# Differential attention: two 64-row score products on the halves of the array in place of one product with a block-diagonal key

## The chip, the core and the metric

The program runs on one core of a Trainium2 chip, as one launch. Its engines are TensorE (PE; PEld is its weight load), VectorE (DVE), ScalarE (ACT), GpSimd (POOL), and SyncE (SP), which here only starts DMAs. Each engine runs its instructions in the order of the program and waits on semaphores for the others. The metric is the device time of one execution in microseconds (us). Of the kernel before there are three runs: 1037.38, 1037.83 and 1040.54 us, with a median of 1037.83 us. One execution was recorded by the hardware profiler; every row below is from that one.

## The reference

The program is three layers deep on 256 tokens of width 1024, all in float32: an attention layer with compressed keys (MLA) and a convolutional FFN, then differential attention and a second FFN, then a hybrid layer. The change lies in the differential attention. Each of its 8 heads has two attention maps of depth 64, and its output is the first map less lambda times the second, times v:

```python
scale = d ** -0.5                                    # d = 64
def block(args):
    qb, qpos = args                                  # 128 queries
    sc = jnp.einsum('bqhjd,bkhjd->bhjqk', qb, k).astype(jnp.float32) * scale
    dist = jnp.abs(qpos[:, None] - pos[None, :]).astype(jnp.float32)
    sc = sc - slopes[None, :, None, None, None] * dist[None, None, None]
    p = jax.nn.softmax(sc, -1)
    a = (p[:, :, 0] - lam * p[:, :, 1]).astype(v.dtype)
    return jnp.einsum('bhqk,bkhd->bqhd', a, v)
o = merge_blocks(lax.map(block, (query_blocks(q), pos.reshape(-1, Q_BLOCK))))
o = rms_norm(o, subln_g) * (1.0 - lam_init)
return o.reshape(b, s, H * 2 * d) @ w_o
```

Here j counts the two maps. The distance term is the same for both.

## The kernel before

Tokens stand in two blocks (tb) of 128. Large products are made by `mm3`: a float32 operand is split into a high and a low part of type float32r, and three matmuls (L131 to L133) sum high by high, high by low and low by high. `wload` brings a weight chunk of 512 KB by DMA (`raw`), casts its high part on ACT (L116) and makes the low part on DVE (L117), in rings of five buffers.

The eight PSUM banks are four accumulators (`acc`, handed out in turn) and four that each layer names by tag. In `diff` these are one `sm`, two `mm` and one `s`. The FFN after it names its own four, two `sm` and two `mm`, over the same four banks: the first use of each waits until the tile that lay there before has been read.

The stage `diff` first makes v for all heads. Then, for each head:

- 48 matmuls of 256 columns make q and k of the head in one `mm` bank (q in the first half, k in the second; 128 rows, 64 of each map).
- ACT copies q to `dq` (L689) and the first map's 64 rows of k into one corner of `kbd` (L691), DVE the second map's rows into the opposite corner (L692). `kbd` holds zeros elsewhere, set once by POOL (L657), so that one product with 128 rows and 512 columns gives both maps' scores.
- For each token block: the score product in the `s` bank (L699, float32, which the profile shows as two matmuls), the distance product on top of it (L700, bfloat16), then `softmax_rows` (maximum L379 on DVE, scaling L380, two exponentials L383 on ACT, reciprocal L385), the two maps joined on DVE (L703 to L705) in `e`, and two transposes of `e` (L707) into the `sm` bank. Below they are called the e transposes.
- When both blocks are there, ACT copies the `sm` bank to `aT` (L708), and four products with v (L711; two matmuls each) add the head's output to `obs`, two accumulators that hold four heads. Below they are called the v products.
- After every fourth head, the outputs are normed: squares on ACT (L719), sums and the inverse root on DVE (L720 to L725), and for each token block four transposes (L173, the o transposes) into `sm`, which ACT and DVE split into `doT` (L127, L128).

Then `wide` multiplies `doT` by the output weights, in accumulators of 512 columns; token block 0 sums in two `acc`, block 1 in `s` and `mm`. `boundary` adds the result to the residual h, a token block at a time (L199, L238 to L244), makes the next norm, and `turn` transposes it for the FFN (L290) into the FFN's two `sm` banks.

The kernel's text does not fix the order of the work on an engine. Tiles are symbolic, and a list scheduler places instructions when their operands and a free buffer are there in its own model of time. While it lets ACT and DVE work on one head's softmax, it places the next head's 48 matmuls on PE, if that head has a bank and weights. Each engine's order is then fixed in the program.

Of the kernel before, what the change touches and what calls it, by code (L numbers as in the profile page):

```python
# [37 lines left out]
def build(tc, a, out):  # L38
# [15 lines left out]
    def banks(c2, **tags):  # L54
        """four banks of a layer, by tag; the other four are accumulators"""
        assert sum(tags.values()) == 4
        uid[0] += 1
        psx[0] = c2.enter_context(tc.tile_pool(name=f"ps{uid[0]}", bufs=1, space=bass.MemoryType.PSUM, reuse_waits="tile"))
        psx[1] = tags
# [40 lines left out]
    tsl = [slice(0, P), slice(P, 2 * P)]  # L100

    def wload(src, n, part=1024, tag="w", hb=HB, pool=None, eng=None, mk=None, scale=None):
        """a weight chunk [128, n]; returns its parts as (high, low) float32r tiles"""
# [36 lines left out]
    def rsqrt(v, n, mul=1.0):  # L140
        """v [P, n] (all positive) -> mul/sqrt(v): bit guess, one tuned and one cubic step."""
# [21 lines left out]
        # y1 is -1/K1 of the first step's value  # L163
# [4 lines left out]
    def tposes(src_list, dst_hi, dst_lo=None, scale=None, eng="v", tag="sm"):  # L168
        """transpose [P,128] pieces into one bank, then move to dst ([P, n, 128] view)."""
# [16 lines left out]
    @contextmanager  # L186
    def behind(*ins):
        """what is traced here goes behind these instructions on their engines"""
        with ExitStack() as c3:
            for e_ in ins:  # L190
                c3.enter_context(tc.issue_after(getattr(e_, "ins", e_)))
            yield
# [9 lines left out]
    def newton(ss, n, width, ins=False, mid=None):  # L202
        """1/sqrt(mean(x^2)+eps) from the scaled sums of one or two parts: bit guess and two Newton
        steps, the first with tuned constants; the sums come scaled so that no factor is left over."""
# [27 lines left out]
    def postnorm(pool, tb, bnk, g_bc):  # L232
        """h += rmsnorm(y) g"""
# [13 lines left out]
    def postnorm_cut(pool, tb, cut, g_bc):  # L247
        """the same for the last token block, in pieces that go out as they are done"""
# [15 lines left out]
    def prenorm(tb, g_bc, aft, warm_):  # L264
        """xT = transpose(rmsnorm(h) g) as high and low parts; 1/rms enters through the transposing product"""
        ss = small(2, F32, "ss2")
        # without a gain here it is in the weights that follow
        hg = [xp.tile([P, 512], F32, tag=f"hg{tb}{f}", name=nm("hg"), bufs=1) if g_bc is not None else h[:, tb, hf[f]] for f in range(2)]
        for f in range(2):
            j_ = square(h[:, tb, hf[f]], D, ss, f)  # L270
            if warm_:
                # keeps the clock of the tensor engine up while it waits
                b_ = smb()
                for _ in range(3):
                    nc.tensor.matmul(b_, j_[:, :P], j_, start=True, stop=True)
# [31 lines left out]
    def boundary(accs, post, pre):  # L307
        """residual add of one sublayer and the norm of the next, a token block at a time;
        returns xT and what is left to do of it, by token block"""
# [34 lines left out]
    def wide(src4, xT, bnk, mk=None, eng=None, hold=(), k0=4, cut=False):  # L344
        """generator: bnk[tb][f] = x @ w, w [1024, 1024] in four chunks of two k tiles; a step is one k tile
        of one token block, the first block's before the second's"""
# [28 lines left out]
    # ================= layer 0: MLA =================  # L375
    def softmax_rows(e, s_ps, n_tb, scale, width=S):
        """s_ps [P, n, w] psum -> e = exp(scale*(s-max)), returns 1/sum [P, n]"""
        mx = small(2, F32, "mx")
        nc.vector.tensor_reduce(mx[:, :n_tb], s_ps, axis=AX.X, op=ALU.max)  # L379
        nc.vector.tensor_scalar(mx[:, :n_tb], mx[:, :n_tb], -scale, None, op0=ALU.mult)  # L380
        sm = small(2, F32, "smx")
        for i in range(n_tb):
            nc.scalar.activation(e[:, i], s_ps[:, i], AF.Exp, bias=mx[:, i:i + 1], scale=scale, accum_out=sm[:, i:i + 1])  # L383
# [4 lines left out]
    def mla(xT, fin):  # L388
        with ExitStack() as c2:
# [10 lines left out]
            # the first two k tiles as plain float32 products  # L400
# [57 lines left out]
            def v_of(tb):                         # tokens on partitions  # L458
# [9 lines left out]
            def qr_of(tb):                        # rope part of q  # L468
# [93 lines left out]
    # ================= conv FFN =================  # L562
    def ffn(li, xT, fin, pre):
        with ExitStack() as c2:
# [6 lines left out]
            # the first two column tiles as plain float32 products, each token block as it comes  # L571
# [67 lines left out]
    # ================= layer 1: differential attention =================  # L639
    def diff(xT, fin):  # L640
        with ExitStack() as c2:
            lp = c2.enter_context(tc.tile_pool(name="diff", bufs=1, reuse_waits="tile"))
            banks(c2, sm=1, mm=2, s=1)
# [11 lines left out]
            kbd = [lp.tile([P, 2, S], F32, tag=f"kbd{i}", name=f"kbd{i}") for i in range(2)]  # L655
            for t in kbd:
                nc.gpsimd.memset(t, 0.0)  # L657
            # v
# [23 lines left out]
            for hd in range(H):  # L682
                wqk = wload(a["diff_qk"][hd], 2048)
                b = mmb().rearrange("p (t s) -> p t s", t=2)
# [3 lines left out]
                q = lp.tile([P, S], F32, tag="dq", name=nm("dq"), bufs=2)  # L688
                nc.scalar.copy(q, b[:, 0])  # L689
                kb = kbd[hd % 2]  # L690
                nc.scalar.copy(kb[0:64, 0], b[0:64, 1])  # L691
                nc.vector.tensor_copy(kb[64:128, 1], b[64:128, 1])  # L692
# [3 lines left out]
                tb_b = smb()  # L696
                for tb in range(2):
                    sb = (mmb() if hd == H - 1 and tb else bank("s")).rearrange("p (t s) -> p t s", t=2)
                    nc.tensor.matmul(sb, q[:, tsl[tb]], kb, start=True, stop=False)  # L699
                    nc.tensor.matmul(sb, sid[:, hd], distb[:, tb:tb + 1, :].to_broadcast([P, 2, S]), start=False, stop=True)  # L700
                    e = lp.tile([P, 2, S], F32, tag="e", name=nm("e"), bufs=2)
                    rs = softmax_rows(e, sb, 2, scale)
# [24 lines left out]
            bs = [[acc(), acc()], [bank("s"), mmb()]]  # L727
# [4 lines left out]
    # ================= hybrid layer =================  # L732
    def hybrid(xT, fin):
        with ExitStack() as c2:
# [48 lines left out]
            oball = Vik                           # o takes the place of v, tokens on partitions  # L783
# [63 lines left out]
            QK = lt("QK", [P, H, 2, S])   # [:, :, 0] = k', [:, :, 1] = q'  (both doubled)  # L847
# [65 lines left out]
            # M[i,j] = -(k_i.k_j) e^(G_i-G_j) c_j for j < i, stored with j on partitions (A) and with i on partitions (M)  # L913
# [47 lines left out]
            # (I - M)^-1 of the 16 x 16 diagonal blocks by substitution, one block on a partition  # L961
# [44 lines left out]
            # blocks of 16 -> 32 -> 64 -> 128; a pair's off-diagonal block lies in the even rows and odd columns  # L1006
# [36 lines left out]
            # outputs, four heads at a time  # L1043
# [44 lines left out]
            def zproj(br, hp):  # L1088
                """(1 + tanh(z/2)) z = 2 silu(z) of two heads"""
# [49 lines left out]
            # rms over each head, with 1/|q| and the 1/2 of silu(z)  # L1139
# [55 lines left out]
    with ExitStack() as c0:  # L1195
        banks(c0, sm=2, mm=2)
        # brings the clock of the tensor engine up while the first loads are on their way
# [13 lines left out]
def _rows(w, kt):  # L1211
    """[kt*128, n] -> [128, kt, n]"""
# [3 lines left out]
def _pairs(w, kt=KT):  # L1216
    """[K, n*256] -> [n, 128, 2, kt, 128]: two column tiles to a chunk"""
# [4 lines left out]
def _ktpairs(w):  # L1222
    """[1024, n] -> [4, 128, 2, n]"""
# [3 lines left out]
def pack(inp):  # L1227
# [10 lines left out]
    # MLA  # L1238
    wa = np.concatenate([f["mla_w_dq"][0], f["mla_w_dkv"][0]], axis=1)
    o["mla_a"] = _ktpairs(wa).reshape(4, P, 1408)  # L1240
    ukv = f["mla_w_ukv"][0].reshape(2, P, H, 2, P)          # kt p h (k|v) d
# [3 lines left out]
    kq = np.concatenate([ukv[:, :, :, 0].transpose(2, 1, 0, 3), uq[:, :, :, :128].transpose(2, 1, 0, 3)], axis=2)   # h p (k2|q3) d  # L1245
# [7 lines left out]
    # FFN  # L1253
# [74 lines left out]
```

## Time and profile before

| What | Value |
|---|---|
| Median of three runs | 1037.83 us |
| Lowest and highest | 1037.38 and 1040.54 us |
| Profiled execution, its span | 1037.8 us |
| PE busy | 1012.7 us, 98% of the span |
| DVE busy | 738.0 us, 71% |
| ACT busy | 545.3 us, 53% |
| Share of PE in the chain that ended last | 84% |

The profiled execution's own time is its span, 1037.8 us, from the first to the last instruction of the one core; it lies on the median. "Busy" counts an engine as busy from the start of an instruction to its end, and ends of matmuls overlap the next, so a busy PE may still be waiting a little. The stage that is changed, from the first head's products to the last products with the output weights, runs from about 346 to 444 us.

### The profile page before, as it was taken

The page shows a single profiled execution, that of the slowest core. Times are in us where ns is not written, and L with a number is a line of the kernel's source. Part 1 is how long each engine was busy: PE and PEld are TensorE (multiplying, and loading weights), DVE is VectorE, ACT ScalarE, POOL GpSimd, SP SyncE. Part 2 cuts the span into 40 slices and gives each one's busy share as a digit, 9 for nine tenths or more (in the row PEclk, how much of TensorE's full clock was granted, in tenths as well). Part 3 has the DMA queues.
Part 4 walks back from the last instruction along what each step waited for, and adds up shares of the span by engine and source line. Part 5 has one row for each costly group of instructions (what it writes and reads, how often), then busy time and mean ns, then how long its engine had stood idle before and what let it go on. Part 6 is the DMA issues. An engine that isn't in the chain of part 4 may idle for free.

```text
span 1037.8 us, 18147 instructions
## 1 busy us (share of the span) xinstructions
PE 1012.7 (98%) x7120; PEld 924.6 (89%) x7120; DVE 738.0 (71%) x1387; ACT 545.3 (53%) x949; POOL 33.1 (3%) x35
## 2 busy tenths in 40 slices
PE   8889899999999999999999999999999999999997
PEld 6778799999987888799999998799898999999996
DVE  5775687777668479778777767578799657685563
ACT  5653466555436456557555554465554455544451
POOL 0000100000012000010000001000203000000000
PEclk9999999999999999999999999999999999999999
DMA  7562467555325425276655442444244413455541
GB/s 276 173 219 81 168 204 222 186 185 179 124 93 189 158 100 172 88 243 234 205 185 187 156 141 76 162 162 164 81 135 102 141 54 113 160 181 185 183 163 41
DMA packets 55301, 162.70 MB, mean 157 GB/s; under 512 B 12784, under 2 KB 15280, under 8 KB 55216
## 3 DMA queue, kind: packets, MB, share of 16 engines
q1 hardware_dynamic: 55216, 161.55, 47.4%
q8 instruction: 56, 0.92, 0.3%
q14 instruction: 29, 0.24, 0.1%
HBM read 160.08 MB, written 1.44 MB: 156 GB/s over the span
## 4 chain that ended last, share of the span: by engine, by line
PE 84%; DVE 9%; ACT 3%; DMA 2%; issue 1%; SPq 0%; POOL 0%; DVEq 0%; ACTq 0%; POOLq 0%
PE mm L131 11%; PE mm L132 11%; PE mm L133 11%; PE acc L132 8%; PE acc L131 8%; PE acc L133 8%; PE sm L133 4%; PE sm L132 4%; PE sm L131 4%; PE mm L583 2%; PE acc L1019 2%; DVE lo L117 1%; PE acc L1054 1%; PE s L699 1%; ACT junk L199 1%
## 5 line engine op out<-in xcount | busy, mean ns | idle before, releaser
L117 DVE TENSOR_TENSOR lo<-raw,hi 128x1024 fp32r<-128x1024 f32 (+1 forms) x271 | 326.5, 1208 | 140.6 <-ACT hi L116 139.4
L116 ACT CAST hi<-raw 128x1024 fp32r<-128x1024 f32 (+1 forms) x271 | 278.2, 1035 | 244.6 <-PE mm L132 126.6
L133 PE MATMUL mm<-xT,lo 128*128 128x256 f32 x928 | 265.6, 286 | 0.0
L131 PE MATMUL mm<-xT,hi 128*128 128x256 f32 x928 | 265.3, 286 | 0.0
L132 PE MATMUL mm<-xT,hi 128*128 128x256 f32 x928 | 264.9, 285 | 0.0
L132 PEld LDWEIGHTS mm<-xT,hi 128*128 128x128 f32 x928 | 177.6, 191 | 1.9 <-issue 0.7
L131 PEld LDWEIGHTS mm<-xT,hi 128*128 128x128 f32 x928 | 177.5, 191 | 1.5 <-issue 0.3
L133 PEld LDWEIGHTS mm<-xT,lo 128*128 128x128 f32 x928 | 177.6, 191 | 1.3 <-issue 0.7
L131 PE MATMUL sm<-xT,hi 128*128 128x256 f32 (+1 forms) x328 | 92.8, 283 | 0.0
L133 PE MATMUL sm<-xT,lo 128*128 128x256 f32 (+1 forms) x328 | 92.8, 283 | 0.0
L132 PE MATMUL sm<-xT,hi 128*128 128x256 f32 (+1 forms) x328 | 92.8, 283 | 0.0
L131 PE MATMUL acc<-hi,gv 128*128 128x512 f32 x176 | 69.2, 393 | 0.0
L132 PE MATMUL acc<-lo,gv 128*128 128x512 f32 x176 | 69.0, 392 | 0.0
L133 PE MATMUL acc<-hi,gv 128*128 128x512 f32 x176 | 68.5, 389 | 0.0
L132 PEld LDWEIGHTS sm<-xT,hi 128*128 128x128 f32 (+1 forms) x328 | 62.2, 190 | 0.9
L131 PEld LDWEIGHTS sm<-xT,hi 128*128 128x128 f32 (+1 forms) x328 | 62.2, 190 | 0.8
L133 PEld LDWEIGHTS sm<-xT,lo 128*128 128x128 f32 (+1 forms) x328 | 62.2, 190 | 0.1
L383 ACT ACTIVATE e<-s,s 128x256 f32<-128x256 f32 x46 | 21.5, 472 | 34.6 <-DVE s L380 32.8
L133 PEld LDWEIGHTS acc<-hi,gv 128*128 128x128 f32 x176 | 33.1, 188 | 7.5 <-DVE gv L125 0.3
L131 PEld LDWEIGHTS acc<-hi,gv 128*128 128x128 f32 x176 | 33.2, 189 | 6.3 <-ACT gv L125 0.6
L132 PEld LDWEIGHTS acc<-lo,gv 128*128 128x128 f32 x176 | 33.2, 189 | 5.3
L131 PE MATMUL mm<-og,hi 128*128 128x256 f32 x128 | 36.0, 281 | 0.0
(462 smaller groups left out, 1905.0 us busy)
## 6 DMA issues: line engine op xcount, KB each, us to landing
raw<-in_ffn_up SPq DMA_DIRECT2D x88, 512.0 KB, 4.6
raw<-in_ffn_down SPq DMA_DIRECT2D x44, 512.0 KB, 4.4
raw<-in_diff_qk SPq DMA_DIRECT2D x16, 512.0 KB, 5.2
raw<-in_h_kq SPq DMA_DIRECT2D x16, 512.0 KB, 4.5
raw<-in_h_qk SPq DMA_DIRECT2D x16, 512.0 KB, 3.9
raw<-in_h_z SPq DMA_DIRECT2D x16, 512.0 KB, 3.7
raw<-in_h_gate SPq DMA_DIRECT2D x16, 512.0 KB, 4.5
raw<-in_h_br SPq DMA_DIRECT2D x16, 512.0 KB, 4.6
```

What stands on the lines that cost most here:

```text
L116: nc.scalar.copy(hi[:, :k], raw[:, :k])
L117: (eng or nc.vector).tensor_tensor(lo[:, :k], raw[:, :k], hi.bitcast(F32)[:, :k], op=ALU.subtract)
L131: nc.tensor.matmul(o, l[0], r[0], start=start, stop=False)
L132: nc.tensor.matmul(o, l[0], r[1], start=False, stop=False)
L133: return nc.tensor.matmul(o, l[1], r[0], start=False, stop=stop)
L199: nc.scalar.activation(junk[:, :p.shape[-1]], p, AF.Square, scale=math.sqrt(beta_of(width)), accum_out=ss[:, i:i + 1])
L383: nc.scalar.activation(e[:, i], s_ps[:, i], AF.Exp, bias=mx[:, i:i + 1], scale=scale, accum_out=sm[:, i:i + 1])
L583: last = nc.tensor.matmul(mmf[j][:, t, tsl[tb]], raws[j][t][:, kt * P:kt * P + P], xF[kt // 4][:, kt % 4, tsl[tb]], start=kt == 0, stop=kt ...
L699: nc.tensor.matmul(sb, q[:, tsl[tb]], kb, start=True, stop=False)
L1019: nc.tensor.matmul(b[:, i], lhs(i), rhs(i), start=True, stop=True)
L1054: nc.tensor.matmul(b[:, i], lhs(hds[i], i), rhs(hds[i], i), start=True, stop=True)
```

## The change

In `diff` the zeros and the block-diagonal `kbd` go. One ACT copy of 512 columns moves q and k to `dqk`. The scores of a head are four products of 64 rows and 256 columns: for each token block, map 0 on the upper half of the array's rows and map 1 on the lower half, each map in a bank of its own, both token blocks beside each other. The distance product is made once per map for both blocks. So a head needs two `s` banks; `mm` gives one up, and heads 1, 3, 5 and 7 make their q and k in an accumulator. `softmax_rows` takes the maximum of each map by itself. At the end, block 1 of the output product sums in the two `s` banks.

```diff
-            banks(c2, sm=1, mm=2, s=1)
+            banks(c2, sm=1, mm=1, s=2)
...
-            kbd = [lp.tile([P, 2, S], F32, tag=f"kbd{i}", name=f"kbd{i}") for i in range(2)]
-            for t in kbd:
-                nc.gpsimd.memset(t, 0.0)
...
-                b = mmb().rearrange("p (t s) -> p t s", t=2)
+                b = (acc if hd % 2 else mmb)().rearrange("p (t s) -> p t s", t=2)
...
-                q = lp.tile([P, S], F32, tag="dq", name=nm("dq"), bufs=2)
-                nc.scalar.copy(q, b[:, 0])
-                kb = kbd[hd % 2]
-                nc.scalar.copy(kb[0:64, 0], b[0:64, 1])
-                nc.vector.tensor_copy(kb[64:128, 1], b[64:128, 1])
+                qk = lp.tile([P, 2, S], F32, tag="dqk", name=nm("dqk"), bufs=2)
+                nc.scalar.copy(qk, b)
...
+                sb = [bank("s").rearrange("p (t s) -> p t s", t=2) for _ in range(2)]
                 for tb in range(2):
-                    sb = (mmb() if hd == H - 1 and tb else bank("s")).rearrange("p (t s) -> p t s", t=2)
-                    nc.tensor.matmul(sb, q[:, tsl[tb]], kb, start=True, stop=False)
-                    nc.tensor.matmul(sb, sid[:, hd], distb[:, tb:tb + 1, :].to_broadcast([P, 2, S]), start=False, stop=True)
+                    for m in range(2):
+                        r = slice(64 * m, 64 * m + 64)
+                        nc.tensor.matmul(sb[m][:, tb], qk[r, 0, tsl[tb]], qk[r, 1], start=tb == 0, stop=False)
+                for m in range(2):
+                    nc.tensor.matmul(sb[m], sid[:, hd], distb, start=False, stop=True)
+                for tb in range(2):
                     e = lp.tile([P, 2, S], F32, tag="e", name=nm("e"), bufs=2)
-                    rs = softmax_rows(e, sb, 2, scale)
+                    rs = softmax_rows(e, [s_[:, tb] for s_ in sb], 2, scale)
...
-            bs = [[acc(), acc()], [bank("s"), mmb()]]
+            bs = [[acc(), acc()], [bank("s"), bank("s")]]
```

And in `softmax_rows`:

```diff
-        nc.vector.tensor_reduce(mx[:, :n_tb], s_ps, axis=AX.X, op=ALU.max)
+        if isinstance(s_ps, list):
+            for i, s_ in enumerate(s_ps):
+                nc.vector.tensor_reduce(mx[:, i:i + 1], s_, axis=AX.X, op=ALU.max)
+        else:
+            nc.vector.tensor_reduce(mx[:, :n_tb], s_ps, axis=AX.X, op=ALU.max)
+            s_ps = [s_ps[:, i] for i in range(n_tb)]
```

Elsewhere the diff only drops comments. Line numbers move: in the changed program the score products are L701, the distance products L703, the e transposes L711, the copy to `aT` L712 and the v products L715.

With other banks the scheduler finds another order. On PE, at head 0, the score and distance products stood in the middle of head 1's matmuls (`mm_3757`):

```order
L131 MATMUL mm_3757<-xT_3313,hi_3747 128x256
L132 MATMUL mm_3757<-xT_3314,hi_3747 128x256
L699 MATMUL s_3706<-kbd_3418,dq_3698 128x512
L700 LDWEIGHTS sid
L700 MATMUL s_3706<-distb,sid 128x512
L133 MATMUL mm_3757<-xT_3313,lo_3748 128x256
```

Now they stand right behind head 0's own matmuls (`mm_3645`), and after them come those of head 2 (`mm_3863`), since head 1 is made later, in an accumulator:

```order
L132 MATMUL mm_3645<-xT_3314,hi_3641 128x256
L133 MATMUL mm_3645<-xT_3313,lo_3642 128x256
L701 MATMUL s_3700<-dqk_3694 128x256
L701 MATMUL s_3701<-dqk_3694 128x256
...
L703 LDWEIGHTS sid
L703 MATMUL s_3700<-distb,sid 128x512
...
L703 MATMUL s_3701<-distb,sid 128x512
L131 MATMUL mm_3863<-xT_3313,hi_3853 128x256
```

The 23 matmuls of the next head that stood between a head's own matmuls and its scores are gone from this place.

On PE, behind the norm of heads 0 to 3, the second o transposes (`on_4095`) were followed by 14 matmuls of a head (`mm_4330`) and a score product before the e transposes of head 4 (`e_4176`, `e_4193`), and the v products stood six matmuls behind these:

```order
L173 MATMUL sm_4097<-c_ident,on_4095 128x128 x4
L131 MATMUL mm_4330<-xT_3313,hi_4320 128x256
...
L699 MATMUL s_4279<-kbd_3419,dq_4273 128x512
L707 MATMUL sm_4172<-c_ident,e_4176 128x128 x2
...
L707 MATMUL sm_4172<-c_ident,e_4193 128x128 x2
L131 MATMUL mm_4330<-xT_3313,hi_4326 128x256
...
L133 MATMUL mm_4330<-xT_3313,lo_4327 128x256
L711 MATMUL acc_4169<-v,aT_4171 128x128 x2
L711 MATMUL acc_4170<-v,aT_4171 128x128 x2
```

Now the second o transposes (`on_4099`), both blocks' e transposes and the v products of head 4 follow each other with nothing between them:

```order
L133 MATMUL mm_4338<-xT_3313,lo_4335 128x256
L173 MATMUL sm_4101<-c_ident,on_4099 128x128 x4
L711 MATMUL sm_4174<-c_ident,e_4183 128x128 x2
L711 MATMUL sm_4174<-c_ident,e_4198 128x128 x2
L715 MATMUL acc_4171<-v,aT_4173 128x128 x2
L715 MATMUL acc_4172<-v,aT_4173 128x128 x2
L131 MATMUL acc_4230<-xT_3313,hi_4220 128x256
```

Each of these groups uses what ACT or DVE makes of the group ahead of it. At heads 0 and 3, too, the v products now stand right behind the e transposes of block 1.

On PE, at the end of the stage, the second norm's first o transposes (`on_4553`) stood 20 output products behind the last v products (`acc_4170`), and eight more stood between them and the second ones (`on_4562`), four of which need nothing of the first ones:

```order
L711 MATMUL acc_4170<-v,aT_4489 128x128 x2
L132 MATMUL s_4573<-lo_4578,doT_3635 128x512
...
L173 MATMUL sm_4555<-c_ident,on_4553 128x128 x4
L133 MATMUL s_4573<-hi_4613,doT_3636 128x512
...
L131 MATMUL acc_4571<-hi_4625,doT_3635 128x512
L132 MATMUL acc_4571<-lo_4626,doT_3635 128x512
...
L173 MATMUL sm_4564<-c_ident,on_4562 128x128 x4
```

Now 13 output products stand there, and four between the two groups of o transposes, all four of which need the first group's `doT`:

```order
L715 MATMUL acc_4172<-v,aT_4497 128x128 x2
L133 MATMUL s_4586<-hi_4601,doT_3632 128x512
...
L173 MATMUL sm_4567<-c_ident,on_4565 128x128 x4
L131 MATMUL acc_4583<-hi_4637,doT_3631 128x512
L132 MATMUL acc_4583<-lo_4638,doT_3631 128x512
L131 MATMUL acc_4584<-hi_4637,doT_3631 128x512
L132 MATMUL acc_4584<-lo_4638,doT_3631 128x512
L173 MATMUL sm_4576<-c_ident,on_4574 128x128 x4
```

The products that stood there have moved ahead of the last v products.

## Rows read from the trace of the kernel before

**Rows 1.** The page, first part: busy time, share of the span, instructions.
```profile
PE 1012.7 (98%) x7120; PEld 924.6 (89%) x7120; DVE 738.0 (71%) x1387; ACT 545.3 (53%) x949; POOL 33.1 (3%) x35
```

**Rows 2.** Stretch of the stage: us, each engine's busy us, granted clock, DMA share.
```profile
346.10:444.00 97.90, 97.09 (x595) 77.53 (x594) 74.91 (x173) 55.00 (x127) 1.07 (x1) 1.00 0.40 134
```

**Rows 3.** Waits of PE from 346 to 444: total us, times, longest.
```profile
PE s L699 <- ACT e L383: 0.2, 1, 0.2
PE sm L707 <- DVE e L705: 0.2, 1, 0.2
```

**Rows 4.** Timeline of PE around a score product: start us, us, engine, line, what.
```profile
387.26 1.06 PE L699 MATMUL s<-kbd,dq 128*128 128x512 f32 x2
388.15 0.38 PE L700 MATMUL s<-distb,sid 128*128 128x512 bf16 x1
...
388.49 0.28 PE L133 MATMUL mm<-xT,lo 128*128 128x256 f32 x1
388.61 0.28 PE L131 MATMUL mm<-xT,hi 128*128 128x256 f32 x1
```

**Rows 5.** Timeline of PE in the hybrid layer, where the array's shape changes.
```profile
835.37 0.28 PE L133 MATMUL mm<-xT,lo 128*128 128x256 f32 x1
835.59 0.67 PE L1019 MATMUL acc<-w,VT 64*64 64x64 f32 x8
836.19 0.68 PE L1019 MATMUL acc<-A,M 128*64 128x64 f32 x8
836.80 0.38 PE L131 MATMUL mm<-xT,hi 128*128 128x256 f32 x1
```

**Rows 6.** Timeline of ACT, behind head 0's matmuls.
```profile
346.17 1.05 ACT L116 CAST hi<-raw 128x1024 fp32r<-128x1024 f32 x1 [1.79 <-PE mm L132]
347.12 0.37 ACT L689 COPY dq<-mm 128x256 f32<-128x256 f32 x1
```

**Rows 7.** Timeline from a head's last e transposes to its v products.
```profile
384.91 0.44 PE L707 MATMUL sm<-c_ident,e 128*128 128x128 f32 x2
385.11 0.36 PE L132 MATMUL mm<-xT,hi 128*128 128x256 f32 x1
...
385.39 0.59 ACT L708 COPY aT<-sm 128x512 f32<-128x512 f32 x1
...
386.03 1.16 PE L711 MATMUL acc<-v,aT 128*128 128x128 f32 x8
```

**Rows 8.** Timeline of PE and DVE, second o transposes of heads 0 to 3.
```profile
396.10 0.66 PE L173 MATMUL sm<-c_ident,on 128*128 128x128 f32 x4
396.76 1.23 DVE L117 TENSOR_TENSOR lo<-raw,hi 128x1024 fp32r<-128x1024 f32 x1 [0.18 <-ACT hi L116]
398.02 0.75 DVE L128 SCALAR_TENSOR_TENSOR doT<-sm,sg,doT 128x512 fp32r<-128x512 f32 x1
```

**Rows 9.** Timeline of PE and DVE, from the last v products on.
```profile
425.96 0.47 PE L132 MATMUL s<-lo,doT 128*128 128x512 f32 x1
...
430.03 1.29 DVE L725 TENSOR_TENSOR on<-acc,s 128x512 f32<-128x512 f32 x2
430.77 0.66 PE L173 MATMUL sm<-c_ident,on 128*128 128x128 f32 x4
...
432.21 0.50 PE L131 MATMUL acc<-hi,doT 128*128 128x512 f32 x1
432.37 0.74 DVE L128 SCALAR_TENSOR_TENSOR doT<-sm,sg,doT 128x512 fp32r<-128x512 f32 x1
```

**Rows 10.** Timeline where the FFN begins: its transposes, and block 1's second half.
```profile
446.00 2.02 PE L290 MATMUL sm<-dg,hg 128*128 128x128 f32 x16 [0.35 <-DVE dg L282]
448.41 0.68 DVE L244 TENSOR_TENSOR yg<-mm,gain 128x512 f32<-128x512 f32 x1
```

**Rows 11.** Busy time by stretch in the first layer, around an idle PE.
```profile
64.40:66.20 1.80, 0.01 (x1) 0.00 (x0) 0.27 (x1) 1.32 (x2) 0.00 (x0) 1.00 0.90 294
67.70:71.10 3.40, 3.40 (x11) 2.81 (x11) 1.33 (x5) 1.60 (x5) 0.00 (x0) 0.50 0.56 183
```

More of the change, by code (lines that the diff above doesn't have):

```diff
@@ L382, in softmax_rows @@
         for i in range(n_tb):
-            nc.scalar.activation(e[:, i], s_ps[:, i], AF.Exp, bias=mx[:, i:i + 1], scale=scale, accum_out=sm[:, i:i + 1])
+            nc.scalar.activation(e[:, i], s_ps[i], AF.Exp, bias=mx[:, i:i + 1], scale=scale, accum_out=sm[:, i:i + 1])
         rs = small(2, F32, "rsx")
```

## The prediction

> **What bounds the kernel now.** I read the page's first part before anything else: PE is busy for 1012.7 of 1037.8 us, DVE for 71% and ACT for 53% of the span [rows 1]. Then I cut out the stage that changes. From 346.1 to 444.0, PE is busy for 97.1 of 97.9 us at the full granted clock, DVE for 74.9 and ACT for 55.0 [rows 2]. The waits of PE in it come to 0.4 us [rows 3]. So the stage is a queue of matmuls without holes. A microsecond less of PE work is a microsecond less of time, and a wait put into that queue costs its full length, since nothing later on PE has slack that could give it back. The end of the program hangs on PE in the same way. The profiled execution took 1037.8 us, the same as the median of the three runs, so I add the terms to that.
>
> The saving is confined to the score products. Whether the order still hides the round trips from PE to ACT or DVE and back decides the sign. I therefore compared the two orders around each round trip, and priced the trips from the timeline.
>
> **a. Scores.** A score product of before is two matmuls of 512 columns; from the first to the distance product behind them it takes 387.26 to 388.15, or 0.89 [rows 4], 0.43 a pass (1.72 a head). The new program has four float32 products of half the columns, eight passes of 0.215, also 1.72 if one follows the other: nothing is saved. If a pass on the upper half runs beside one on the lower, at best four slots remain: 0.86 a head, 6.9 for eight heads. In program order both passes of map 0 come before those of map 1; if only neighbours on different halves overlap, eight passes fill five slots of 0.215, 1.08. That saves 0.64 a head, 5.1 in all, and I take it. The distance products keep their columns: two of 512 before, two of 512 now. Each change of the array's shape costs something: in the hybrid layer the step into 64x64 tiles takes 0.22 (835.37 to 835.59) [rows 5] where products of this size stand 0.12 apart (388.49 to 388.61) [rows 4]. That is 0.1; the step from 64x64 to 128x64 cannot be told from the eight matmuls around it. With 0.09 for each of 16 changes 1.4 goes back. Net −3.7; the ends are −6.9 and +1.4.
>
> The Trainium skill, "TensorE: Matmul & The Clock Gate", Part 3, says that tiles on different row groups overlap, while matmuls start and end in order. By it the five slots hold; without it the sum would be 5.1 higher. No row of this trace has two halves at work. Another page of the Trainium skill speaks against the change: "TensorEngine Tiling (Array Packing)", Key Properties, has a change of tiling mode drain the engine. Worked out from that, a drain costs what a matmul still has to run when the next would start, 0.28 − 0.12 = 0.16 [rows 4], so 16 of them 2.6 and the sum 1.2 higher; this is an estimate. The 0.1 of [rows 5] is smaller, and decides.
>
> **b. Head 0.** Its scores used to stand 23 matmuls behind its own products; now nothing is between. The last product starts at 346.17 − 0.2 or so; ACT first finishes the weight cast that is ahead in its queue (346.17, next ACT work at 347.12) and then copies q and k in one copy of 512 columns [rows 6]. Such a copy takes 0.59 [rows 7]. With 0.1 for the semaphore PE starts at 347.8 instead of 346.2: **+1.6** (0.8 if the cast is not in front, 1.9 at most).
>
> **c. The v products** of heads 0, 3 and 4 now stand right behind the e transposes. Before, from e transposes to v products was 384.91 to 386.03 with the `aT` copy inside it and other matmuls to fill it: 1.12, less 0.20 for the transposes themselves [rows 7]. So 0.9 is bare in each of three heads, 2.7. In heads 0 and 4 a cast of 1.05 [rows 6] can stand in front of the copy; I add 0.8 and 0.3 for parts of it: **+3.8** (1.5 to 4.5).
>
> **d. Head 4.** With the one `sm` bank the e transposes cannot begin until `doT` of the second o transposes has been read out. These began at 396.10, and DVE finished with the bank at 398.02 + 0.75 = 398.77, behind a low part of 1.23 [rows 8]. Of the 2.67, 0.45 is PE's own transposing; 2.2 was filled by 14 matmuls of the next head and is bare now. One more cast may stand ahead on ACT: **+2.5** (2.2 to 2.9). Queued behind the waiting transposes are the v products and then head 5's matmuls, so all of PE stops.
>
> **e. The tail.** From the last v products to the first o transposes runs a chain of ACT squares and the inverse root on DVE: 425.96 to 430.77, with `on` written at 430.03 [rows 9]. Twenty output products covered it, 0.24 each. Thirteen cover 3.1: 1.7 bare. Next come output products that need the new `doT`; these ran at 432.21, 1.44 after the transposes' start, less 0.42 for the transposes: 1.0 bare, where four other products stood. The second o transposes wait until DVE has read the bank (432.37 + 0.74) [rows 9], with four products of 0.24 as cover: 1.0 again. **+3.7** (2.0 to 5.0).
>
> **f. Start of the FFN.** Its transposing banks lie over the stage's banks. Block 1 of the output product now ends in both `s` banks, so the second bank of transposes waits for the read of block 1's second half. That read ran at 448.41 + 0.68 = 449.1; the second eight of the 16 transposes began about 446.00 + 1.0 = 447.0 [rows 10]. DVE's order there is the same as before, so PE waits: **+2.0** (0.4 if DVE is early against a PE that is late by then).
>
> **g. Small waits.** In heads 1, 2, 5, 6 and 7 fewer matmuls of another head are at hand, but some are: **+1.0** (0 to 3). PE's own old waits of 0.4 [rows 3] go with the old order.
>
> **h. The clock.** Bare waits let PE go idle. In the first layer PE was idle from 64.40 to 66.20, and then the granted clock was 0.50 (1.2 of 2.4 GHz) from 67.70 to 71.10 [rows 11]: 3.4 us at half speed, a loss of 1.7. The waits of b, d and e are of that length. I take one such fall: **+1.7** (0 to 5).
>
> **At nothing** I put the rest. ACT loses 16 small copies and gets 8 of 0.59. DVE loses eight copies and splits its maxima in two. POOL loses its two memsets. ACT and DVE have 43 and 23 us free in the stage [rows 2], and PE hides them; where it does not, b to f have charged it. The transfers and SP's queue keep their order.
>
> Sum: −3.7 + 1.6 + 3.8 + 2.5 + 3.7 + 2.0 + 1.0 − 0.4 + 1.7 = +12.2, or **1050.0 us**.
>
> **Rivals.**
> *The halves run one after the other.* Then a is +1.4: the sum is 17.3, 1055. For it: no row shows overlap. Against: the two halves use different rows, weights and banks. 17%.
> *The clock falls at b, d and e.* Two more falls of 1.7: 15.6, 1053 to 1056. For it: three waits of 1.6 or more; against: the idle time of [rows 11] is as long as the longest of them, and most waits are shorter. 10%.
> *Half of the waits stay hidden,* because ACT and DVE do casts early while PE waits, so that later round trips find empty queues. Of the 14.6 of b to g some 7 remain, no fall of the clock: −3.7 + 7.3 − 0.4, about 1041 to 1042. For it: the slack of [rows 2]. Against: the trips in c and e start only from what PE has just made. 9%.
> *The other side: faster.* All halves pair up and the changes of shape cost nothing (−6.9), and the wait at head 0 puts ACT and DVE ahead for good, so that only b and 1.0 of e remain: −6.9 + 1.6 + 1.0 − 0.4 = −4.7, 1033. It decides when the waits sum to less than what the scores save. Against: DVE is 77% busy in the stage, and d and f are not about who is ahead, but about one bank. 4%.
> My forecast has 60%.
>
> **Range and chances.** The half widths of the terms (a 4.1, b 0.5, c 1.5, d 0.4, e 1.5, f 0.8, g 1.5, h 2.5), taken as independent, give ±5.6. Down that and a little of the third rival is 1043; up, the first two rivals with a larger part of the waits reach 1059. A measurement tells 0.3%, 3.1 us, from no change: 1034.7 to 1040.9. Faster takes most of the last rival, 3%; within it falls the lower part of the third and the rest of the last, 5%; slower 92%.
>
> **What would show it.** Right: PE's waits in the stage rise from 0.4 to about 14 us, with the score products of head 0, the v products of heads 0, 3 and 4, the e transposes of head 4, both groups of o transposes and the FFN's transposes as the waiting lines; a score group of four products takes about 1.1 us; outside the stage nothing moves. Wrong: score groups of 1.7 us (a), no wait of over 2 us at head 4 (d), a stage that waits for less than 6 us in all, or a granted clock under 1 for over 4 us.

## The result, and the profile after

The changed kernel took 1054.53 us in the median of four executions (1051.03 to 1061.56), against 1037.96 (1037.38 to 1040.54, four) of the kernel before: a ratio of 1.0163, with a 95% interval of 1.0135 to 1.0190. A second series on another occasion gave 1057.07 (1053.02 to 1061.29, six) against 1039.86, a ratio of 1.0156 (1.0128 to 1.0184). The change is a loss of some 17 us; +12.2 was forecast, to 1050.0, in a range of 1043 to 1059.

The time of an execution is some 2.0 us above its span (1061.56 to 1059.5, 1037.49 to 1035.5). The profiled execution of before, with a span of 1037.8, therefore stood near 1039.9 and not on the median as I had taken it; set against that, the sum of the prediction would have come to 1052. Below, spans are compared with spans.

First the waits of PE in the changed kernel, from the start of head 0's scores to the FFN's first products (what waits, for whom, total us, times, longest). In the kernel before this view had two lines of 0.2 for the stage [rows 3], and 0.4 at the FFN's start [rows 10].

```profile
PE acc L715 <- ACT aT L712: 2.5, 3, 1.0
PE sm L711 <- DVE doT L128: 2.5, 1, 2.5
PE sm L173 <- DVE on L729: 2.3, 2, 1.6
PE s L701 <- ACT dqk L691: 1.5, 1, 1.5
PE sm L290 <- DVE yg L244: 1.5, 1, 1.5
PE sm L711 <- DVE e L709: 1.1, 2, 0.9
PE sm L290 <- DVE yg L238: 1.0, 1, 1.0
PE sm L173 <- DVE doT L128: 0.9, 1, 0.9
PE acc L131 <- ACT doT L127: 0.8, 1, 0.8
```

They come to 14.1 us, and most name a place of the prediction: the v products behind `aT` (c), head 4's e transposes behind `doT` (d), the tail's transposes and first output product (e), head 0's scores (b), the FFN's transposes (f). The rest, 1.1 for `e` and 0.7 of the 2.3 for `on`, are small waits (g).

The granted clock is the second part of the loss. These are stretches of the changed kernel (us, busy us of PE, PEld, DVE, ACT and POOL, granted clock, share and GB/s of the DMA):

```profile
400.90:407.50 6.60, 5.61 (x25) 5.21 (x26) 2.71 (x3) 2.68 (x3) 0.00 (x0) 0.51 0.50 164
445.20:448.50 3.30, 3.27 (x10) 2.73 (x11) 3.30 (x4) 0.69 (x1) 0.00 (x0) 0.54 0.84 261
462.20:465.70 3.50, 2.86 (x13) 2.90 (x14) 1.84 (x3) 1.05 (x3) 1.27 (x1) 0.54 0.57 152
813.90:824.30 10.40, 10.40 (x50) 9.97 (x49) 5.43 (x16) 2.55 (x6) 1.51 (x1) 0.51 0.04 7
```

In each of them the clock stands at the lower of its two levels, 1.2 of 2.4 GHz. The first three begin at or behind the waits of head 4, of the tail and of the FFN's start. The fourth lies in the hybrid layer, which is unchanged, behind a wait of 1.8 us that the kernel before has too, there without a fall (first the changed kernel, then the one before):

```profile
PE acc L1023 <- DVE A L988: 1.8, 1, 1.8
PE acc L1019 <- DVE A L984: 1.8, 1, 1.8
```

To compare the stages I took the stretch from the warming products (L275) ahead of the stage to the FFN's first product behind it, and for the lost clock the sum over pieces of 1 us of one less the granted clock. These three columns are of one profiled execution each. The last column is of all executions whose clock is listed: the mean of the span times its mean granted clock, an estimate of the length of the whole program at full clock. Like the lost clock, it counts time in which PE was idle as well.

| Kernel | Stretch, us | Lost clock | At full clock | Whole program at full clock (executions) |
|---|---|---|---|---|
| before | 136.6 | 0.0 | 136.6 | 1034.4 (17), 1033.8 (23) |
| changed | 151.8 | 6.2 | 145.6 | 1043.6 (4) |
| changed, again | 151.5 | 6.2 | 145.2 | 1043.7 (6) |
| one half of the rows for both maps | 156.0 | 6.8 | 149.2 | 1046.6 (4) |
| only the banks changed | 151.0 | 4.0 | 147.0 | 1044.3 (4) |
| only the products changed | 138.4 | 0.0 | 138.4 | 1034.7 (12) |
| FFN's bank undone | 147.4 | 3.4 | 143.9 | 1040.4 (4) |
| head 4's wait filled | 147.1 | 1.7 | 145.4 | 1043.3 (6) |
| products in closed groups | 138.1 | 1.7 | 136.4 | 1033.8 (12) |
| the same, output banks exchanged | 135.3 | 0.0 | 135.3 | 1032.3 (12) |

So in all executions the changed kernel is 9 to 10 us longer at full clock; the other 6 to 7 us of the loss are about what the clock lost more. The profiled executions are not typical in this second part: both of the changed kernel were the slowest of their series. Of the 22 us between the spans of the first and of before (1059.5 less 1037.8), 9.0 are the stage at full clock, 6.2 its lost clock, 5.75 lost clock behind it, and 1.7 more lost clock ahead of it (3.4 against 1.7); the program's end and the unchanged stages give back 0.9. The clock that was lost outside the stage is not of every execution: spans of the four run from 1049.0 at a mean granted clock of 0.995 to 1059.5 at 0.984.

### The profile page after: what moved, and what is told of

It reads as the page before. It is cut to its first block, busy times and chain, and to the rows that moved or that the text cites. A ratio compares the mean times of both kernels' runs of the same rounds, so it can differ in the third digit from the quotient of the medians.

```text
span 1059.5 us, 18207 instructions
## 1 busy us (share of the span) xinstructions
PE 1020.5 (96%) x7152; PEld 936.7 (88%) x7152; DVE 735.5 (69%) x1395; ACT 545.8 (52%) x941; POOL 32.5 (3%) x33
## 4 chain that ended last, share of the span: by engine, by line
PE 82%; DVE 10%; ACT 3%; DMA 2%; issue 1%; SPq 0%; POOL 0%; DVEq 0%; ACTq 0%; POOLq 0%
PE mm L132 11%; PE mm L131 11%; PE mm L133 11%; PE acc L132 8%; PE acc L131 8%; PE acc L133 8%; PE sm L133 4%; PE sm L132 4%; PE sm L131 4%; PE mm L588 3%; PE acc L1023 2%; DVE lo L117 2%; PE acc L1058 1%; PE sm L290 1%; ACT hi L116 1%
## 5 line engine op out<-in xcount | busy, mean ns | idle before, releaser
L131 PE MATMUL mm<-xT,hi 128*128 128x256 f32 x864 | 247.7, 287 | 0.0
L133 PE MATMUL mm<-xT,lo 128*128 128x256 f32 x864 | 247.0, 286 | 0.0
L132 PE MATMUL mm<-xT,hi 128*128 128x256 f32 x864 | 246.8, 286 | 0.0
L132 PEld LDWEIGHTS mm<-xT,hi 128*128 128x128 f32 x864 | 165.9, 192 | 1.5 <-issue 0.3
L131 PEld LDWEIGHTS mm<-xT,hi 128*128 128x128 f32 x864 | 165.8, 192 | 1.4
L133 PEld LDWEIGHTS mm<-xT,lo 128*128 128x128 f32 x864 | 165.9, 192 | 0.5
L131 PE MATMUL acc<-xT,hi 128*128 128x256 f32 x128 | 37.3, 292 | 0.0
L132 PE MATMUL acc<-xT,hi 128*128 128x256 f32 x128 | 37.3, 291 | 0.0
```

Source lines behind the costliest of these rows:

```text
L131: nc.tensor.matmul(o, l[0], r[0], start=start, stop=False)
L132: nc.tensor.matmul(o, l[0], r[1], start=False, stop=False)
L133: return nc.tensor.matmul(o, l[1], r[0], start=False, stop=stop)
```

## The experiments

**Do the halves run side by side?** Both maps' products were put on the upper half of the rows; map 1's scores are left out.

```diff
-                        r = slice(64 * m, 64 * m + 64)
+                        r = slice(0, 64)
```

> Both maps' score products take the upper half of the rows, so map 1's scores are left out and map 0's stand twice. Banks, shapes, counts and order stay. Theory (halves side by side): a group of four products, 1.07 us in the changed kernel's trace (367.30 to 368.37), rises to 8 passes of 0.215 = 1.72, and with eight groups the time rises by some 5 us over the changed kernel, to about 1059. Rival (the halves run one after another anyway): the group stays at 1.07, the time at about 1054.

A score group of the changed kernel, then the same group here (start us, us, engine, line, what):

```profile
367.30 1.13 PE L701 MATMUL s<-dqk 64*128 64x256 f32 x8
368.37 0.60 PE L703 MATMUL s<-distb,sid 128*128 128x512 bf16 x2
```

```profile
367.30 1.99 PE L701 MATMUL s<-dqk 64*128 64x256 f32 x8
369.22 0.60 PE L703 MATMUL s<-distb,sid 128*128 128x512 bf16 x2
```

The group takes 1.92 instead of 1.07. The difference, 0.85, is four passes of 0.215: on two halves eight passes fill four slots, and 0.2 is left for the two changes of shape. So where the halves run side by side, they do so completely. Only four of the changed kernel's eight groups look like this one; in the other four the products of one half started 0.24 to 0.41 us behind those of the other, and the group took 1.30 to 1.58. One of them:

```profile
372.75 1.37 PE L701 MATMUL s<-dqk 64*128 64x256 f32 x8
374.05 0.39 PE L703 MATMUL s<-distb,sid 128*128 128x512 bf16 x1
```

On one half every group takes 1.92 at full clock, 15.4 in all against 10.1, or 5.3 us more. The stage at full clock is 3.6 longer, because the waits shrank from 14.1 to 12.5: the 0.7 for `on` of the first norm and the tail's 0.9 for `doT` are gone. The time, 1056.96 (1054.87 to 1059.59), lies between the changed kernel's two medians, and the 1059 expected did not show: the difference is smaller than the changing loss of clock. In the table's last column it is there, 3.0 us.

**Banks alone.** The kernel before with the new banks: its block-diagonal key and its 512-column products stay.

```diff
-            banks(c2, sm=1, mm=2, s=1)
+            banks(c2, sm=1, mm=1, s=2)
-                b = mmb().rearrange("p (t s) -> p t s", t=2)
+                b = (acc if hd % 2 else mmb)().rearrange("p (t s) -> p t s", t=2)
-                    sb = (mmb() if hd == H - 1 and tb else bank("s")).rearrange("p (t s) -> p t s", t=2)
+                    sb = bank("s").rearrange("p (t s) -> p t s", t=2)
-            bs = [[acc(), acc()], [bank("s"), mmb()]]
+            bs = [[acc(), acc()], [bank("s"), bank("s")]]
```

> The kernel before with its block-diagonal key and 512-column products, but with the new allotment of banks (one mm, two s, odd heads' q and k in an accumulator, block 1 of the output in the two s banks). Theory (the loss lies in the banks and the order that follows from them, not in the products): PE's waits in the stage rise from 0.4 to 12 us or more, and the time lies 12 to 18 us above before, at 1050 to 1056, although no 64-row product is there. Rival (the loss comes from the row-tiled products, their shape changes or their copies): the time stays within 4 us of before, under 1042.

1054.36 us, a ratio of 1.0138 (1.0110 to 1.0165): nearly the whole loss, without one 64-row product, and within the 1050 to 1056 expected. The waits come to 11.4 us in the stage and at the FFN's start, a little under the 12 expected. The longest of PE are those of the changed kernel at the same places (L699 stands for L701, L707 for L711, L711 for L715):

```profile
PE s L699 <- DVE kbd L692: 2.7, 1, 2.7
PE sm L707 <- DVE doT L128: 2.2, 1, 2.2
PE acc L711 <- ACT aT L708: 1.8, 2, 1.1
PE sm L290 <- DVE yg L244: 1.6, 1, 1.6
```

The stage at full clock is 10.4 us longer than before; the new products give back 1.4 of that. The loss lies in the banks and the order that follows from them. No run kept these banks with another order, so how much of it a better order would win back stays open.

**Products alone.** The reverse: the new products on the banks of before, with map 1's scores in an accumulator.

```diff
-            banks(c2, sm=1, mm=1, s=2)
+            banks(c2, sm=1, mm=2, s=1)
-                b = (acc if hd % 2 else mmb)().rearrange("p (t s) -> p t s", t=2)
+                b = mmb().rearrange("p (t s) -> p t s", t=2)
-                sb = [bank("s").rearrange("p (t s) -> p t s", t=2) for _ in range(2)]
+                sb = [b_.rearrange("p (t s) -> p t s", t=2) for b_ in (bank("s"), acc())]
-            bs = [[acc(), acc()], [bank("s"), bank("s")]]
+            bs = [[acc(), acc()], [bank("s"), mmb()]]
```

> The new products with the banks of before (two mm, one s; q and k of every head in mm; block 1 of the output in s and mm); the second map's scores go to an accumulator. Theory: with the second mm bank back PE finds other heads' matmuls to fill the round trips, its waits in the stage fall from 14 to about 3 us, and the saved 3 to 5 us of scores make up for them: 1035 to 1040. Rival (the products themselves lose): waits fall but the time stays above 1045.

1040.29 us (12 executions) against 1040.52, a ratio of 1.0003 (0.9990 to 1.0016), just above the 1035 to 1040 expected. The waits fall to 1.9 us with the FFN's start (1.1 for xF, 0.4 for dg, 0.4 for on), but of the 3 to 5 us that the scores were to save almost nothing is left. Here is PE at head 0 and at the next head:

```profile
346.57 0.28 PE L131 MATMUL mm<-xT,hi 128*128 128x256 f32 x1
346.80 0.48 PE L701 MATMUL s<-dqk 64*128 64x256 f32 x1
346.80 0.48 PE L701 MATMUL acc<-dqk 64*128 64x256 f32 x1
347.12 0.38 PE L701 MATMUL s<-dqk 64*128 64x256 f32 x1
347.12 0.38 PE L701 MATMUL acc<-dqk 64*128 64x256 f32 x1
347.33 0.38 PE L701 MATMUL s<-dqk 64*128 64x256 f32 x1
347.34 0.38 PE L701 MATMUL acc<-dqk 64*128 64x256 f32 x1
347.55 0.38 PE L701 MATMUL s<-dqk 64*128 64x256 f32 x1
347.56 0.38 PE L701 MATMUL acc<-dqk 64*128 64x256 f32 x1
347.86 0.39 PE L703 MATMUL s<-distb,sid 128*128 128x512 bf16 x1
...
354.62 1.13 PE L701 MATMUL s<-dqk 64*128 64x256 f32 x4
355.67 1.16 PE L715 MATMUL acc<-v,aT 128*128 128x128 f32 x8
356.76 1.13 PE L701 MATMUL acc<-dqk 64*128 64x256 f32 x4
357.82 0.39 PE L703 MATMUL s<-distb,sid 128*128 128x512 bf16 x1
```

At head 0 the passes of the two maps start in pairs at the same instant, four slots of 0.215, 1.06 from the first to the distance product. At the next head the scheduler set four passes of one half here and four of the other two us later: 1.05 and 1.06, twice the price. The two banks come free at different times there; that this is why it split them is argued, not shown. Summed from each record's start to the next matmul's, the 64 score records of this stage take 14.8 us, those of the changed kernel 10.1 and the 32 of before 15.15. The gain hangs on the four products standing together, which the kernel's text does not say.

**The FFN's bank.** In the changed kernel block 1's second half sums in `mm` again.

```diff
-            bs = [[acc(), acc()], [bank("s"), bank("s")]]
+            bs = [[acc(), acc()], [bank("s"), mmb()]]
```

> The changed kernel with one edit: the second half of output block 1 sums in mm, as before, not in s. Theory: the wait of 1.5 us of the FFN's transposes for yg (L244) goes, 1.0 for the other half may stay, other waits stay at about 11.6; the time is 1 to 2 us under the changed kernel, and if the clock does not fall at the FFN's start 1 to 2 us more. Rival (the FFN's transposes wait for something that comes as late): nothing changes by over 0.5 us there.

The wait for L244 is gone and the one of 0.9 for L238 stays, as expected; all waits come to 12.1, since the tail's transposes now wait 0.7 longer. The stage at full clock is 1.7 us shorter (143.9). In its profile the clock no longer falls at the FFN's start. It does not fall behind head 4 either, although the wait there is as long as in the changed kernel; the one fall, of 6.8 us, lies behind the tail's longer wait:

```profile
397.83 0.66 PE L711 MATMUL sm<-c_ident,e 128*128 128x128 f32 x4 [2.50 <-DVE doT L128]
```

```profile
397.50:404.50 7.00, 6.00 (x49) 5.76 (x50) 3.04 (x4) 4.05 (x5) 0.00 (x0) 1.00 0.50 168
```

1052.00 us (1048.60 to 1057.38), 2.5 under the changed kernel's first median, but the executions of both overlap. At full clock the whole program is 3.2 us shorter.

**The clock.** The changed kernel ran once more; beside it, one with ten products of the identity, whose result nobody reads, in the wait of head 4.

```diff
+                if hd == 4:
+                    with behind(*tr):
+                        fill = [nc.tensor.matmul(obs[0][:, 3 * P:], ident, ident, start=True, stop=True) for _ in range(10)]
...
+                      with behind(*(fill if hd == 4 else ())):
                         nc.tensor.transpose(tb_b
```

Here `tr` is the last of the o transposes.

> The changed kernel once more, so that the next three have it on the same chip. At full clock its stage took 9 us longer than before; what lies above that is clock. Theory (the falls of the clock follow from the waits): every execution shows some, and its spans lie 9 us plus the lost clock over before, the mean granted clock at 0.984 to 0.995 against 0.995 to 0.999. Rival (the falls are of single executions and not of this kernel): the mean granted clock is as high as in the kernel before and the time falls to about 1046.

> The changed kernel with ten products of 128 columns, whose result nobody reads, in the wait of head 4 between the second o transposes and the e transposes (some 2.0 of the 2.5 us). They lengthen nothing that PE could have done. Theory (the wait's price is its length and a fall of the clock behind it): the wait for doT falls from 2.5 to about 0.5, the stage at full clock stays as long, and the fall of the clock behind head 4 (0.50 from 401 to 408 in the changed kernel's trace, 3.3 us lost) goes: 1 to 3 us less than the changed kernel, not as low as before. Rival (the clock falls there for another reason): the clock falls at head 4 as it did, and the time stays.

The repeat, 1057.07 us, has every wait listed above within 0.1 us, and its clock falls at the same four places (0.50 from 401 to 407, 446 to 448, 463 to 465 and 814 to 823). Its six executions have mean granted clocks of 0.986 to 0.994, those of before 0.990 to 0.999, so the theory held and the time did not fall to 1046. The filled kernel took 1051.19 us (1048.55 to 1053.38), 5.9 less. PE in its wait, and its granted clock behind it:

```profile
394.85 0.60 PE L175 MATMUL sm<-c_ident,on 128*128 128x128 f32 x4
395.28 2.40 PE L702 MATMUL acc<-c_ident 128*128 128x128 f32 x20
397.95 0.66 PE L717 MATMUL sm<-c_ident,e 128*128 128x128 f32 x4 [0.27 <-DVE doT L128]
```

```profile
400.00:407.00 7.00, 7.00 (x61) 7.00 (x61) 3.59 (x3) 3.94 (x4) 0.00 (x0) 1.00 0.56 172
436.50:440.30 3.80, 2.99 (x9) 2.09 (x10) 3.80 (x5) 0.65 (x2) 0.00 (x0) 0.61 0.41 119
```

The fall behind head 4 is gone; the one behind the tail's unfilled waits stays. This one trace does not show that the filling did it, since with the FFN's bank undone the fall was missing too, behind an unfilled wait; and the execution profiled here was the fastest of its six. The executions together show it: the program at full clock is as long as the changed kernel's (1043.3 and 1043.7), so all the gain is clock, with a mean over six executions of 0.9945 against 0.9895. The kernel with the FFN's bank undone has 0.9905, no more than the changed one. The gain is larger than the 1 to 3 us expected: in the profiled execution the clock fell neither at the FFN's start nor in the hybrid layer. Whether those two hang on the fall at head 4 or went by chance stays open.

**Closed groups.** The distance products go first and start the banks, and the four score products stand behind both; the banks are those of the products alone. In a second kernel the output's blocks exchange their banks as well.

```diff
-                for m in range(2):
-                    nc.tensor.matmul(sb[m], sid[:, hd], distb, start=False, stop=True)
+                ds_ = [nc.tensor.matmul(sb[m], sid[:, hd], distb, start=True, stop=False) for m in range(2)]
+                with behind(*ds_):
+                    for tb in range(2):
+                        for m in range(2):
+                            r = slice(64 * m, 64 * m + 64)
+                            nc.tensor.matmul(sb[m][:, tb], qk[r, 0, tsl[tb]], qk[r, 1], start=False, stop=tb == 1)
```

And in the second kernel alone:

```diff
-            bs = [[acc(), acc()], [bank("s"), mmb()]]
+            bs = [[bank("s"), mmb()], [acc(), acc()]]
```

> As the kernel with the new products on the banks of before, but the distance products stand ahead of the score products (they start the banks), and the four score products of a head are held behind both, so that halves 0 and 1 stand side by side. Theory (the products alone gained nothing because the scheduler split the groups of four into pairs on the same half, 14.8 us for the 64 records against 10.1 in the changed kernel): the 64 records fall to 9 to 10.5 us and the time to 2 to 5 us under before, about 1034 to 1038. Rival (a gain of PE there is lost to waits for ACT and DVE whatever the order): the records get shorter, waits grow by as much, and the time stays within 1 us of before.

> As the kernel before it in this list, with the output product's banks exchanged: block 0 sums in s and mm, block 1 in two accumulators, so that the FFN's transposing banks are not those of the block that is read last. Theory: the FFN's transposes and its first products wait up to 1 us less than there; 0 to 1.5 us below it. Rival (those waits are for the norm's chain on DVE, not for a bank): no difference of over 0.5 us.

The 64 records fell to 10.4 and 10.0 us, as expected, 5 under before. The times, 1038.96 and 1039.00, have ratios of 0.9988 (0.9973 to 1.0002) and 0.9992 (0.9972 to 1.0011): no difference that can be told, so the theory's 2 to 5 us missed. The stage at full clock is 0.2 and 1.3 us under before. New waits took most, 5.1 and 3.9 us against 0.8 before, so the rival fits better; the longest of the first kernel:

```profile
PE sm L711 <- DVE e L709: 2.7, 4, 2.0
PE mm L588 <- ACT xF L298: 1.1, 1, 1.1
PE sm L173 <- DVE on L729: 0.7, 2, 0.6
```

The longest one, in the middle of the stage, goes back over DVE and ACT to a transfer. A weight cast on ACT (first row) waited 2.40 us for it; DVE's low part followed, and DVE's work on the scores (L385) stood behind that in its queue:

```profile
403.70 1.05 ACT L116 CAST hi<-raw 128x1024 fp32r<-128x1024 f32 x1 [2.40 <-DMA raw<-in_diff_o]
```

```profile
404.78 1.23 DVE L117 TENSOR_TENSOR lo<-raw,hi 128x1024 fp32r<-128x1024 f32 x1 [1.56 <-ACT hi L116]
405.92 0.16 DVE L385 TENSOR_SCALAR s<-s 128x2 f32<-128x2 f32 x1
408.11 0.48 DVE L709 SCALAR_TENSOR_TENSOR e<-e,s 128x256 f32<-128x256 f32 x1
```

In the second kernel the FFN's wait of 1.1 is gone, as its theory said, and the longest wait for `e` is 1.0. By the table's last column it is 1.5 us shorter than before at full clock, but no version of the study beats the kernel before in time.

## Why the prediction held, and where its sum was off

**a.** Right in sign, too small: −3.7 forecast, −5.0 measured (15.15 to 10.1). The new products came out as forecast, 8 × 1.08 + 1.4 = 10.1, but by luck. I had reckoned with five slots in every head. Where the products of both halves start together there are four, since the passes of a float32 product on one half do not hold back those of the other; in four heads one half started late, and the groups took 1.30 to 1.58. The two errors cancel. What was missing is on the other side: I had priced the old products at 0.43 a pass, 0.86 each, after one place, where already 0.89 stood [rows 4]; over all 16 it was 0.95. The 0.1 for a change of shape holds, going in (346.57 to 346.80, where 0.12 is usual) and out (347.55 to 347.86, where 0.215 is). So the 0.16 that I worked out from the Trainium skill's rule on drains ("TensorEngine Tiling (Array Packing)", Key Properties) is not borne out; its rule of overlap ("TensorE: Matmul & The Clock Gate", Part 3) agrees with the starts 0.01 apart, and the five slots were my reading of it.

**b to g.** 14.6 forecast, 14.1 measured; the places were right, but the sum is this close because single terms missed by up to 1.3 in both directions. Head 0: 1.6, measured 1.5. v products: 3.8, measured 2.5 at the same three heads; the 1.1 that I had added for casts did not come. Head 4: 2.5 and 2.5. The tail: 3.7, measured 3.3 (1.6, 0.8 and 0.9, each at its place). The FFN: 2.0, measured 2.5, in two waits where I had one: the first transposes too waited, 1.0, for the read of block 1's first half. Small waits: 1.0, measured 1.8 (0.7 for `on` of the first norm, 1.1 for `e`).

**At full clock** the terms without h gave +10.5; the stage shows +9.0 and, again, +8.6. The rows agree with that: 14.1 of waits where 0.8 were before, less 5.0 of scores, is 8.3. The experiment with the banks alone confirms that this is the banks and the order; with the products alone the whole program at full clock is within 0.3 us of before (the one profiled stretch is 1.8 longer), so the products by themselves cost next to nothing.

**h.** This is the term that was mis-sized: one fall of 1.7 forecast, in a range of 0 to 5, and 6 to 7 us of lost clock measured over all executions. In both profiled executions the stage and the FFN's start lost 6.2, by three falls, of which the first lost 3.4 and so lasted 6.8 us, twice the length of the one in [rows 11]. My own sign of being wrong, a granted clock under 1 for over 4 us, therefore came true for this term. I had argued against several falls with the idle time of [rows 11], "as long as the longest" of the waits; it is 1.8, and my wait at head 4 was 2.5. The rival with falls at b, d and e (10%) came nearest: d and e it had right; at b the changed kernel's two profiles show none, those of two experiments do (from 346.4 with both maps on one half, from 348.5 with the banks alone), and the FFN's start fell as well. The measured differences, 16.6 and 17.2, stand 4 to 5 us above the forecast 12.2: more lost clock than I had, in part offset by 1 to 2 us less at full clock. That the time lies inside the range is in part luck, since the lost clock was above h's own range and the other terms came out lower.

The rival on the other side and the one with half of the waits hidden are refuted by the waits; that the halves run one after another by the first experiment.

## What to carry to other kernels

When a change takes a buffer from one stage to give it to another, list what could run ahead because of that buffer; here the new allotment, with one of two `mm` banks given up, cost 10 us of waits, and of clock some 6 more (a mean granted clock of 0.9895 against 0.9958 in the second series), against 5 us of saved matmuls. Price bare waits of PE at their length, and add lost clock: here waits of 1.5 to 2.5 us were followed by falls in some executions and not in others, so it takes several executions to see the price. Where a wait can't be removed, idle products can fill it; here they took 5.9 us off. A gain from two products side by side exists only where the program's order sets them side by side: tie them together and look at their start times.

## What the runs showed of the hardware that was not expected

Two float32 products of 64 rows on the two halves start within 0.01 us of each other and take no longer than one (0.215 a pass of 256 columns). Falls of the clock to 0.50 lasted some 3.4, 6.8 or 10.2 us (twice the clock that they lost: 1.7, 3.4 and 5.1), and one wait did not always bring the same: behind the 2.5 us at head 4 the clock fell for 6.8 in the changed kernel, for 3.4 with both maps on one half, and not at all with the FFN's bank undone. The longest fall lies in an unchanged layer with PE busy throughout, behind the wait of 1.8; both profiled executions of the changed kernel had it, two of the eight other profiles had one of 3.4 there (from 796.1 with the products alone, from 794.6 with the output banks exchanged), six none. Lost clock also spread the executions of one kernel over 10 us, while its waits, in the two that were profiled, repeated within 0.1 us.
